# New durations in the cost table of a list schedule, with the instructions kept

## The chip, the cores and the metric

The kernel runs on one core of a Trainium2 chip. The metric is the device time of one execution in microseconds: 1900.26 us is the median of three runs of the kernel before, which lie between 1900.05 and 1903.23 us.

## The reference

The program is a whole network for one batch of 256 tokens of width 1024, all in fp32. The first half has two hybrid layers (in the kernel's names L0 and L1), the second half two blocks of feed-forward nets around a mixer. Cut to what matters:

```python
# each of the two hybrid layers
hx = rms_norm(x, norm_w) * (1 + scale_x) + shift_x           # scale, shift, gate: c_silu @ ada_w
hy = rms_norm(y, norm_w) * (1 + scale_y) + shift_y           # y: 256 tokens of context
p, cp = hx @ w_in, hy @ w_in
ret_x = head_group_norm(bidir_retention(...)) * silu(rg)     # branch r: 4 heads
na_x  = neighbourhood_attention(...) * silu(ng)              # branch n: 8 heads
gqa_x = gqa_blocks(axial_rope(rms_norm(q)), ...) * silu(gg)  # branch g: 8 query heads
x = x + gate_x * ((sig(m0) * (ret_x @ w_ret_o) + sig(m1) * (na_x @ w_na_o)
                   + sig(m2) * (gqa_x @ w_gqa_o)) @ w_out)
y = ...                                                       # the same for the context, layer 0 only
# second half, two blocks: h + 0.5 * swiglu(rms_norm(h)) ; h + mixer(rms_norm(h)) ; the same again
```

## The kernel before

All matrix products are fp32 in three passes: each operand is split into a rounded part and a rest (`split`: a copy on ScalarE makes the rounded part, a subtraction on VectorE the rest), and TensorE multiplies part by part, part by rest and rest by part (`mm3`). A weight comes by DMA into a tile `raw` of 128x2048, and is split into tiles `wh` (ScalarE) and `wl` (VectorE), of which there are four each. Activations lie in 60 tiles `r`, results of TensorE in 8 tiles `ps`, one bank each. The names of tiles begin with a stage and end with a running number: `L0g_r_847` is a tile `r` of branch g in layer 0, `L0m_ps` a sum of the merge of the branches (`m`: gates and output products), `L1r` branch r of layer 1, `ada` the products that give scale, shift and gate, `pro` the start, `f`, `fb`, `fa`, `f0b` and their like the feed-forward nets, `mix` the mixers. The running numbers shift by one or two when the order of recording shifts.

A head or a pair of heads of a branch is a generator (a task). The stages of one in branch g: products for q; the mean of squares by a product with ones; square root on ScalarE, `RECIPROCAL` on VectorE; the scaled q (`SCALAR_TENSOR_TENSOR ...<-L0g_ps,vecs,L0g_r`); a permutation by TensorE (`L0g_ps<-L0g_r,cstt`) and three operations of VectorE that make the rotation; scores; softmax on ScalarE, VectorE and, for the sums over partitions, GpSimd; the split of the probabilities; the product with the values (`L1g_ps<-L1g_r,L1gk_r`).

The order of the program is not the order in which the code is written. Every instruction is recorded first (`record`, line 146), with a duration that `cost` (line 116) works out from its shape. TensorE's durations are also summed into `now`, in the order of recording; a task that says `yield 14` goes on when `now` has moved by 14. Then a list schedule (`schedule`, line 187) makes the order. Each instruction has a due time: where `now` stood when it was recorded, plus 25 for an engine other than TensorE, and never later than the due time of what needs it, less its own duration and 0.6 (line 195). Going through a time of its own, the schedule gives each engine that is free the ready instruction with the earliest due time; an instruction is ready 0.15 after its last source has ended (line 314), and tiles, a ScalarE table that must be loaded (1.28, line 285) and DMAs in flight hold it back as well. `issue` (line 327) emits the instructions in the order so found; line 335, which every row of the profile names, is the call in it. Each engine then works through its own list in that order, and waits on semaphores for what a tile needs.

Of the kernel before, what the change touches and what calls it, by code (L numbers as in the profile page):

```python
# [7 lines left out]
F32 = mybir.dt.float32  # L8
# [87 lines left out]
class _Recorder:  # L96
# [19 lines left out]
    def cost(self, eng, method, out, ins, kw):  # L116
        n = 1
        for e in out.shape[1:]:
            n *= e
        psum = any(i.space == bass.MemoryType.PSUM for i in ins) or out.space == bass.MemoryType.PSUM  # L120
        if eng == "tensor":
            rhs = ins[-1]
            n = 1
            for e in rhs.shape[1:]:
                n *= e
            d = max(n, 64) / 2400.0 * (4 if rhs.dtype == F32 and method == "matmul" else 1) + 0.002
            return d * 0.31 if out.shape[0] == 32 else d
        if eng == "scalar":
            return (n + (61 if psum else 112)) / 1200.0 + 0.093 * (len(ins) - 1)
        if eng == "vector":  # L130
            per = {"reciprocal": 6.0, "tensor_tensor_scan": 2.0}.get(method, 1.0)
            if method == "tensor_scalar" and not psum:
                per = 0.5
            if method == "tensor_reduce":
                n = 1
                for e in ins[0].shape[1:]:
                    n *= e
            return (66 + per * n) / 960.0 + (0.06 if method == "scalar_tensor_tensor" and len(ins) == 3 else 0)
        if eng == "gpsimd":
            return 0.38 + 7.5 * n / 1200.0 if method == "partition_all_reduce" else 0.09 + n / 1200.0  # L140
        b = 4
        for e in out.shape:
            b *= e
        return b / 360e3
# [1493 lines left out]
```

## Time and profile before

| | |
|---|---|
| median of the runs | 1900.26 us |
| profiled execution | 1902.64 us, its span 1900.9 us |
| mean granted TensorE clock | 0.994 |
| TensorE busy | 1858.4 us, 98% of the span |
| VectorE busy | 1432.9 us, 75% |
| ScalarE busy | 1066.3 us, 56%, of it 71.8 us in 56 table loads |
| GpSimd busy | 209.7 us, 11% |
| DMA | 291.95 MB, 152 GB/s read |

A row of a timeline is one instruction or a run of like ones; a number in brackets is the time for which the engine stood idle before it, with the instruction that ended the wait. A windows row gives the busy time of each engine in a stretch, and the granted clock of TensorE in it, where 1.00 is 2.4 GHz and 0.50 is 1.2 GHz.

### The profile page before, as it was taken

Reading aid. Unit: us, or ns where it says so; the run is one execution under the profiler, and the core shown is the slowest. Engines: PE = TensorE matmul, PEld = TensorE weight load, DVE = VectorE, ACT = ScalarE, POOL = GpSimd, SP = SyncE. Lnnn points to the kernel's source line nnn. Section 1 sums busy time; section 2 is a strip of 40 time slices with the busy share of each in tenths; the row PEclk is TensorE's granted clock in tenths of the full one; section 3 lists DMA queues with packets and bytes.
Section 4 is the critical chain, followed back from the end, with each engine's and each line's share of the span. In section 5 each row is a group of like instructions: output and inputs, shape, how many; then the busy total and the mean of one; then the engine's idle time right before and its main releaser. Section 6 shows DMA issues by size and latency. Waiting matters only on the chain.

```text
span 1900.9 us, 33415 instructions
## 1 busy us (share of the span) xinstructions
PE 1858.4 (98%) x13632; PEld 1739.5 (92%) x13632; DVE 1432.9 (75%) x2177; ACT 1066.3 (56%) x1704; POOL 209.7 (11%) x152
## 2 busy tenths in 40 slices
PE   6999999999999999999999999999999999999998
PEld 4888777777789889999999999999999999999998
DVE  7778978799857699999787668876656665777654
ACT  4656555656445597766565447754445444755443
POOL 0123323133300022222000000000000010000000
PEclk9999999999999999999999999999999999999999
DMA  9332443524343324434655566355555555545552
GB/s 321 119 97 93 128 148 101 155 88 123 102 153 100 89 78 116 124 106 146 209 178 188 190 194 200 111 201 187 179 183 180 188 181 193 190 157 176 181 188 98
DMA packets 336249, 291.95 MB, mean 154 GB/s; under 512 B 9184, under 2 KB 325728, under 8 KB 336096
## 3 DMA queue, kind: packets, MB, share of 16 engines
q1 hardware_dynamic: 336096, 289.82, 48.0%
q8 instruction: 107, 1.75, 0.4%
q14 instruction: 46, 0.38, 0.1%
HBM read 288.75 MB, written 1.05 MB: 152 GB/s over the span
## 4 chain that ended last, share of the span: by engine, by line
PE 87%; DVE 8%; ACT 2%; issue 1%; POOL 1%; DMA 0%; SPq 0%; DVEq 0%; POOLq 0%; ACTq 0%
PE fb_ps L335 13%; PE L0m_ps L335 7%; PE f_ps L335 7%; PE fa_ps L335 7%; PE L0n_ps L335 5%; PE L1m_ps L335 5%; PE L1r_ps L335 4%; PE L0r_ps L335 4%; PE fb1b_ps L335 3%; PE L1n_ps L335 3%; PE fa1b_ps L335 3%; PE fb0b_ps L335 3%; PE f0b_ps L335 3%; PE mix_ps L335 3%; PE L0out_ps L335 2%; PE L0in_ps L335 2%
## 5 line engine op out<-in xcount | busy, mean ns | idle before, releaser
L335 PE MATMUL fb_ps<-fb_r,fb_wh 128*128 128x256 f32 x1408 | 253.8, 283 | 0.0
L335 PEld LDWEIGHTS fb_ps<-fb_r,fb_wh 128*128 128x128 f32 x1408 | 219.6, 192 | 0.1
L335 PE MATMUL fb_ps<-fb_r,fb_wl 128*128 128x256 f32 x704 | 198.9, 283 | 0.0
L335 ACT CAST fb_wh<-fb_raw 128x1024 fp32r<-128x1024 f32 x88 | 92.2, 1047 | 123.0 <-PE fb_ps L335 89.3
L335 DVE TENSOR_TENSOR fb_wl<-fb_raw,fb_wh 128x1024 fp32r<-128x1024 f32 x88 | 107.7, 1224 | 65.1 <-ACT fb_wh L335 65.0
L335 PEld LDWEIGHTS fb_ps<-fb_r,fb_wl 128*128 128x128 f32 x704 | 135.0, 192 | 0.0
L335 PE MATMUL f_ps<-f_r,f_wh 128*128 128x256 f32 x704 | 127.2, 283 | 0.0
L335 PE MATMUL fa_ps<-fa_r,fa_wh 128*128 128x256 f32 x704 | 126.9, 283 | 0.0
L335 PE MATMUL L0m_ps<-L0in_r,L0m_wh 128*128 128x512 f32 x384 | 121.5, 395 | 0.0
L335 PEld LDWEIGHTS f_ps<-f_r,f_wh 128*128 128x128 f32 x704 | 109.8, 192 | 0.1
L335 PEld LDWEIGHTS fa_ps<-fa_r,fa_wh 128*128 128x128 f32 x704 | 109.8, 192 | 0.1
L335 PE MATMUL fa_ps<-fa_r,fa_wl 128*128 128x256 f32 x352 | 99.4, 283 | 0.0
L335 PE MATMUL f_ps<-f_r,f_wl 128*128 128x256 f32 x352 | 99.3, 283 | 0.0
L335 PEld LDWEIGHTS L0m_ps<-L0in_r,L0m_wh 128*128 128x128 f32 x384 | 71.9, 189 | 16.7 <-issue 1.6
L335 ACT CAST fa_wh<-fa_raw 128x1024 fp32r<-128x1024 f32 x44 | 46.1, 1047 | 63.5 <-PE fa_ps L335 39.7
L335 DVE TENSOR_TENSOR fa_wl<-fa_raw,fa_wh 128x1024 fp32r<-128x1024 f32 x44 | 53.8, 1224 | 35.4 <-ACT fa_wh L335 35.4
L335 POOL MEMSET mix_r<- 128x128 f32 (+1 forms) x36 | 7.7, 239 | 653.4 <-DVE fa_r L335 490.4
L335 DVE TENSOR_TENSOR L0g_r<-L0g_r,L0g_r 128x512 f32<-128x512 f32 (+3 forms) x116 | 72.4, 670 | 7.6 <-ACT L0g_r L335 5.4
L335 ACT CAST f_wh<-f_raw 128x1024 fp32r<-128x1024 f32 x44 | 46.1, 1048 | 56.4 <-PE f_ps L335 35.6
L335 PE MATMUL L0m_ps<-L0in_r,L0m_wl 128*128 128x512 f32 x192 | 75.0, 391 | 0.0
L335 ACT ACT_TABLE_LOAD x56 | 71.8, 1283 | 3.1 <-PE L0out_ps L335 1.4
L335 DVE TENSOR_TENSOR f_wl<-f_raw,f_wh 128x1024 fp32r<-128x1024 f32 x44 | 53.7, 1221 | 24.9 <-ACT f_wh L335 24.8
(506 smaller groups left out, 5729.7 us busy)
## 6 DMA issues: line engine op xcount, KB each, us to landing
fb_raw<-in_ffn_w_in_dram SPq DMA_DIRECT2D x44, 1024.0 KB, 5.2
f_raw<-in_ffn_w_in_dram SPq DMA_DIRECT2D x22, 1024.0 KB, 5.1
fa_raw<-in_ffn_w_in_dram SPq DMA_DIRECT2D x22, 1024.0 KB, 5.2
ada_raw<-in_ada_w_dram SPq DMA_DIRECT2D x32, 512.0 KB, 4.5
L0m_raw<-in_w_in_dram SPq DMA_DIRECT2D x24, 512.0 KB, 3.9
L1m_raw<-in_w_in_dram SPq DMA_DIRECT2D x24, 512.0 KB, 4.3
L0in_raw<-in_ada_w_dram SPq DMA_DIRECT2D x32, 256.0 KB, 6.0
f0b_raw<-in_ffn_w_out_dram SPq DMA_DIRECT2D x8, 1024.0 KB, 5.3
```

The costliest lines, as they stand in the source:

```text
L335: getattr(getattr(self.real, eng), method)(*a, **k)
```

## The change

Five constants of `cost` change; nothing else does. For TensorE a matmul was reckoned at its columns by 2.4 GHz and 2 ns, and is now reckoned at its columns by 2.4 GHz and 13.5 ns, at least 109 ns: 256 columns go from 0.109 to 0.120, 512 columns from 0.215 to 0.227. An operation of ScalarE gets 118 cycles more on SBUF and 109 more on PSUM, 0.098 and 0.091 us: a copy of 1024 columns goes from 0.947 to 1.045. An operation of VectorE gets 84 cycles more, 0.0875 us: a subtraction of 1024 columns goes from 1.135 to 1.223.

```diff
-            d = max(n, 64) / 2400.0 * (4 if rhs.dtype == F32 and method == "matmul" else 1) + 0.002
-            return d * 0.31 if out.shape[0] == 32 else d
+            if out.shape[0] == 32:
+                return max(n, 64) / 2400.0 * 0.5 + 0.002
+            return max(n / 2400.0 * (4 if rhs.dtype == F32 and method == "matmul" else 1) + 0.0135, 0.109)
         if eng == "scalar":
-            return (n + (61 if psum else 112)) / 1200.0 + 0.093 * (len(ins) - 1)
+            return (n + (170 if psum else 230)) / 1200.0 + 0.093 * (len(ins) - 1)
...
-            return (66 + per * n) / 960.0 + (0.06 if method == "scalar_tensor_tensor" and len(ins) == 3 else 0)
+            return (150 + per * n) / 960.0 + (0.06 if method == "scalar_tensor_tensor" and len(ins) == 3 else 0)
```

The set of instructions stays, but for table loads of ScalarE, 59 where there were 56. Their order moves on every engine, about a third of TensorE's list and more than half of VectorE's.

The first place is VectorE's list in layer 0, around the `RECIPROCAL` of the third group of branch g (`L0g_r_847`). Before:

```order
L335 SCALAR_TENSOR_TENSOR L0m_r_804<-L0m_r_804,L0m_ps_824 128x512
L335 TENSOR_TENSOR L0g_r_820<-L0g_r_820,L0g_r_811 128x256
L335 TENSOR_TENSOR L0m_m_481<-L0m_m_481,L0m_r_804 128x512
L335 TENSOR_TENSOR L0m_wl_865<-L0m_raw_863,L0m_wh_864 128x512
L335 SCALAR_TENSOR_TENSOR L0m_r_829<-L0m_r_829,L0m_ps_832 128x512
L335 RECIPROCAL L0g_r_847<-L0g_r_847 128x512
L335 TENSOR_TENSOR L0m_wl_887<-L0m_raw_884,L0m_wh_886 128x1024
L335 SCALAR_TENSOR_TENSOR L0g_r_848<-L0g_ps_834,vecs,L0g_r_847 128x512
L335 TENSOR_TENSOR L0m_m_495<-L0m_m_495,L0m_r_829 128x512
```

Now:

```order
L336 TENSOR_TENSOR L0g_r_819<-L0g_r_819,L0g_r_810 128x256
L336 TENSOR_TENSOR ada_90<-ada_r_820,vecs 128x8
L336 TENSOR_TENSOR L0g_r_819<-L0g_r_819,L0g_r_810 128x256
L336 RECIPROCAL L0g_r_847<-L0g_r_847 128x512
L336 TENSOR_TENSOR ada_90<-ada_r_820,vecs 128x8
L336 SCALAR_TENSOR_TENSOR L0m_r_803<-L0m_r_803,L0m_ps_824 128x512
L336 SCALAR_TENSOR_TENSOR L0g_r_848<-L0g_ps_834,vecs,L0g_r_847 128x512
L336 TENSOR_TENSOR L0m_m_482<-L0m_m_482,L0m_r_803 128x512
L336 TENSOR_TENSOR L0m_wl_863<-L0m_raw_861,L0m_wh_862 128x512
```

The `RECIPROCAL` stood behind a rest of a weight (`L0m_wl_865`) and two scaled additions of the merge; now it stands right behind the sum of the exponentials of the group before, with two short ada additions at its sides, and the weight's rest behind the scaled q.

The second place is VectorE's list at the end of layer 0, where the last group of branch g is divided by its sums: `L0g_r_1002` is the group's output, `L0g_r_957` (now `L0g_r_955`) the reciprocal of the sums, `L0g_r_1004` the rest of the product that TensorE waits for. Before:

```order
L335 TENSOR_TENSOR L0g_r_1002<-L0g_ps_997,L0g_r_1002 64x512
L335 TENSOR_TENSOR L0m_wl_1019<-L0m_raw_1016,L0m_wh_1018 128x1024
L335 TENSOR_TENSOR L0m_m_709<-L0m_m_709,L0m_r_987 128x512
L335 TENSOR_TENSOR L0m_wl_1022<-L0m_raw_1010,L0m_wh_1021 128x512
L335 RECIPROCAL L0g_r_957<-L0g_r_957 128x512
L335 TENSOR_TENSOR L0g_r_1002<-L0g_ps_1001,L0g_r_1002 64x512
L335 SCALAR_TENSOR_TENSOR L0g_r_957<-L0g_r_957,L0g_r_917 128x512
L335 SCALAR_TENSOR_TENSOR L0m_r_996<-L0m_r_996,L0m_ps_1000 128x512
L335 TENSOR_TENSOR L0g_r_1002<-L0g_r_1002,L0g_r_957 128x512
L335 TENSOR_TENSOR L0m_m_742<-L0m_m_742,L0m_r_996 128x512
L335 TENSOR_TENSOR L0m_wl_1029<-L0m_raw_1026,L0m_wh_1028 128x1024
L335 TENSOR_TENSOR L0g_r_1004<-L0g_r_1002,L0g_r_1003 128x512
```

Now:

```order
L336 TENSOR_TENSOR L0g_r_1002<-L0g_ps_997,L0g_r_1002 64x512
L336 TENSOR_TENSOR L0g_r_1002<-L0g_ps_1001,L0g_r_1002 64x512
L336 TENSOR_TENSOR L0m_wl_1012<-L0m_raw_1010,L0m_wh_1011 128x512
L336 RECIPROCAL L0g_r_955<-L0g_r_955 128x512
L336 SCALAR_TENSOR_TENSOR L0m_r_987<-L0m_r_987,L0m_ps_991 128x512
L336 SCALAR_TENSOR_TENSOR L0g_r_955<-L0g_r_955,L0g_r_915 128x512
L336 TENSOR_TENSOR L0m_m_709<-L0m_m_709,L0m_r_987 128x512
L336 TENSOR_TENSOR L0g_r_1002<-L0g_r_1002,L0g_r_955 128x512
L336 TENSOR_TENSOR L0m_wl_1019<-L0m_raw_1016,L0m_wh_1018 128x1024
L336 TENSOR_TENSOR L0g_r_1004<-L0g_r_1002,L0g_r_1003 128x512
L336 TENSOR_TENSOR L0m_wl_1022<-L0m_raw_1010,L0m_wh_1021 128x512
L336 SCALAR_TENSOR_TENSOR L0m_r_996<-L0m_r_996,L0m_ps_1000 128x512
```

The two rests `L0m_wl_1019` and `L0m_wl_1022` stood ahead of the `RECIPROCAL`; now they stand behind the multiplication, and `L0m_wl_1012` alone stands ahead.

The third place is TensorE's list in layer 1, where the scores of the second group of branch g end (`L1g_ps_1381`) and the first group's product with the values begins (`L1g_ps_1389<-L1g_r_1352,L1gk_r_1309`). Before:

```order
L335 MATMUL L1g_ps_1381<-L1g_r_1358,L1gk_r_1302 128x256
L335 MATMUL L1g_ps_1381<-L1g_r_1356,L1gk_r_1302 128x256
L335 MATMUL L1g_ps_1381<-L1g_r_1358,L1gk_r_1302 128x256
L335 MATMUL L1g_ps_1381<-L1g_r_1356,L1gk_r_1302 128x256
L335 MATMUL L1r_ps_1397<-L0out_r_1156,L1r_wh_1398 128x256
L335 MATMUL L1r_ps_1397<-L0out_r_1157,L1r_wh_1398 128x256
L335 MATMUL L1r_ps_1397<-L0out_r_1156,L1r_wl_1399 128x256
L335 MATMUL L1r_ps_1397<-L0out_r_1159,L1r_wh_1398 128x256
```

Now:

```order
L336 MATMUL L1g_ps_1381<-L1g_r_1358,L1gk_r_1302 128x256
L336 MATMUL L1g_ps_1381<-L1g_r_1356,L1gk_r_1302 128x256
L336 MATMUL L1g_ps_1381<-L1g_r_1358,L1gk_r_1302 128x256
L336 MATMUL L1g_ps_1381<-L1g_r_1356,L1gk_r_1302 128x256
L336 MATMUL L1g_ps_1389<-L1g_r_1352,L1gk_r_1309 128x256
L336 MATMUL L1r_ps_1397<-L0out_r_1156,L1r_wl_1399 128x256
L336 MATMUL L1r_ps_1397<-L0out_r_1159,L1r_wh_1398 128x256
L336 MATMUL L1r_ps_1397<-L0out_r_1160,L1r_wh_1398 128x256
L336 MATMUL L1r_ps_1397<-L0out_r_1159,L1r_wl_1399 128x256
```

Before, 51 matmuls of branch r (`L1r_ps`) stood between the last score and the first product with the values, of which the first four are shown; now that product follows the last score at once, and those of branch r stand behind it.

## Rows read from the trace of the kernel before

**Rows 1.** The page, section 1: busy time, share of the span, instructions.

```profile
PE 1858.4 (98%) x13632; PEld 1739.5 (92%) x13632; DVE 1432.9 (75%) x2177; ACT 1066.3 (56%) x1704; POOL 209.7 (11%) x152
```

**Rows 2.** Waits of PE: what was waited for, total us, times, longest us.

```profile
PE pro_ps L335 <- DVE pro_r L335: 12.3, 1, 12.3
PE L0g_ps L335 <- DVE L0g_r L335: 4.7, 2, 3.6
PE L0m_ps L335 <- ACT L0g_r L335: 3.8, 1, 3.8
PE L1g_ps L335 <- ACT L1g_r L335: 2.9, 3, 1.9
...
PE L0n_ps L335 <- DVE L0n_r L335: 2.0, 3, 1.0
...
PE mix0yb_ps L335 <- DVE mix0y_r L335: 1.0, 1, 1.0
```

**Rows 3.** Chain of waits in order of time: start us, us, what.

```profile
692.67 7.44 PE L1r_ps L335 x51
...
1243.67 127.14 PE fb_ps L335 x1058
```

**Rows 4.** Windows: length; busy us of PE, PEld, DVE, ACT, POOL; PEclk; DMA, GB/s.

```profile
330.00:430.00 100.00, 96.31 (x485) 73.22 (x486) 88.26 (x119) 61.97 (x96) 25.86 (x12) 0.98 0.39 123
430.00:508.00 78.00, 73.12 (x355) 58.79 (x354) 73.81 (x102) 46.51 (x75) 32.37 (x8) 1.00 0.34 101
747.00:894.00 147.00, 145.50 (x1108) 140.06 (x1107) 143.74 (x246) 102.39 (x187) 35.27 (x26) 1.00 0.41 121
326.00:332.00 6.00, 4.53 (x22) 3.51 (x21) 5.94 (x6) 3.19 (x4) 0.00 (x0) 1.00 0.00 0
422.00:426.00 4.00, 4.00 (x21) 2.52 (x14) 4.00 (x4) 0.00 (x0) 0.00 (x0) 0.57 0.97 338
507.50:511.00 3.50, 2.95 (x7) 2.37 (x8) 2.18 (x3) 0.99 (x2) 0.00 (x0) 0.51 0.18 51
690.00:695.00 5.00, 5.00 (x25) 5.00 (x25) 4.34 (x12) 4.31 (x10) 2.43 (x2) 0.50 0.63 176
```

**Rows 5.** Timeline of DVE, 775 to 790 us: start us, us, instruction.

```profile
784.84 1.21 DVE L335 TENSOR_TENSOR L1n_wl<-L1n_raw,L1n_wh 128x1024 fp32r<-128x1024 f32 x1
785.98 0.68 DVE L335 TENSOR_TENSOR L1m_wl<-L1m_raw,L1m_wh 128x512 fp32r<-128x512 f32 x1
```

**Rows 6.** Timeline of ACT, 775 to 790 us.

```profile
782.40 1.05 ACT L335 CAST L1n_wh<-L1n_raw 128x1024 fp32r<-128x1024 f32 x1
783.35 0.61 ACT L335 CAST L1m_wh<-L1m_raw 128x512 fp32r<-128x512 f32 x1
```

**Rows 7.** Timeline of DVE, 409 to 422 us.

```profile
412.74 2.73 DVE L335 TENSOR_TENSOR L0m_wl<-L0m_raw,L0m_wh 128x512 fp32r<-128x512 f32 x1
...
415.99 3.34 DVE L335 RECIPROCAL L0g_r<-L0g_r 128x512 f32<-128x512 f32 x1
...
420.33 0.73 DVE L335 SCALAR_TENSOR_TENSOR L0g_r<-L0g_ps,vecs,L0g_r 128x512 f32<-128x512 f32 x1
```

**Rows 8.** Timeline of PE, 408 to 426 us; in brackets the idle time before.

```profile
421.21 0.67 PE L335 MATMUL L0g_ps<-L0g_r,cstt 128*128 128x256 f32 x2 [3.55 <-DVE L0g_r L335]
```

**Rows 9.** Timeline of DVE, 492 to 512 us.

```profile
501.24 3.33 DVE L335 RECIPROCAL L0g_r<-L0g_r 128x512 f32<-128x512 f32 x1
...
506.66 0.68 DVE L335 TENSOR_TENSOR L0g_r<-L0g_r,L0g_r 128x512 f32<-128x512 f32 x1
```

**Rows 10.** Timeline of PE, 490 to 512 us.

```profile
508.05 0.80 PE L335 MATMUL L0m_ps<-L0g_r,L0m_wh 128*128 128x512 f32 x1 [3.82 <-ACT L0g_r L335]
```

**Rows 11.** Timeline of PE, 692 to 712 us.

```profile
699.95 0.28 PE L335 MATMUL L1g_ps<-L1g_r,L1gk_r 128*128 128x256 f32 x1
```

**Rows 12.** Timeline of ACT, 674 to 702 us.

```profile
684.72 0.58 ACT L335 COPY L1g_r<-L1g_ps 128x512 f32<-128x512 f32 x1
...
698.72 1.13 ACT L335 CAST L1g_r<-L1g_r 128x512 fp32r<-128x512 f32 x2
```

## Prediction

> **What bounds the kernel now.** I read the page first. TensorE is busy for 1858.4 of 1900.9 us, so at most 42.5 us of the span are not its own work [rows 1]. The chain of waits shows where nothing can be won: a feed-forward stretch is 127.14 us for 1058 matmuls of 256 columns, 0.1202 us each with no wait inside [rows 3], and four such stretches and their output halves fill most of the time after 950 us. The order of back-to-back matmuls is worth nothing, so what the change does is decided where TensorE waits. The waits view lists these places [rows 2]: 12.3 us before the first matmul, then branch g of layer 0 (4.7 us in two waits, 3.6 the longest, and 3.8 at its end), branch g of layer 1 (2.9), branch n (2.0) and the first mixer (1.0). The windows add a second price: behind a long wait TensorE's granted clock falls to 1.2 GHz. From 422 to 426 it was 0.57 of full speed, a loss of 0.43 x 4 = 1.7 us of work, and from 507.5 to 511 it was 0.51, again 1.7 us. Behind the 1.47 us that are missing between 326 and 332 (4.53 of 6 us busy) it stayed at 1.00 [rows 4]. So a wait of 3.5 us costs about 5.2, and one of 1.5 costs only itself.
>
> The instructions are the same, so the sum below has only waits in it, read by what stands ahead of what in the new lists, at the durations of the trace.
>
> **First place, third group of branch g in layer 0.** TensorE stands idle for 3.55 us until 421.21, for the scaled q [rows 8]; it had run out of work at 421.21 - 3.55 = 417.66. On VectorE the scaled q starts at 420.33, behind the reciprocal (3.34 us from 415.99) and a weight's rest, and the reciprocal itself starts behind another rest that took 2.73 us from 412.74 [rows 7]. In the new list both rests stand behind the scaled q. From 412.74 to 415.99 are 3.25 us, from the reciprocal's end (415.99 + 3.34 = 419.33) to 420.33 is 1.0: without them the scaled q starts near 420.33 - 4.25 = 416.1, and a scaled addition that now stands in between gives back 0.6. It ends (0.73) near 417.4, before TensorE runs out. The wait goes, and with it the slow stretch: -3.55 - 1.7 = -5.2 us. Bounds: -5.3, and -2 if ScalarE's square root comes later than it did.
>
> **Second place, end of layer 0.** TensorE waits 3.82 us until 508.05 for the split product [rows 10]. On VectorE the reciprocal starts at 501.24 and the multiplication at 506.66 [rows 9]. The new list takes the rests 1019 and 1022 and one scaled addition out of this path, but keeps one other rest in it, and the first addition cannot start before its product is there; I count 1.4 us earlier. TensorE's list has five more matmuls of 512 columns to do meanwhile, at twice the spacing of rows 3 about 1.2 us. So 3.82 - 2.6 = 1.2 us remain, which by the window from 326 to 332 is too little for the clock to fall: -2.6 - 1.7 = -4.3. Bounds: -5.5 (nothing remains), -1.4 (only the path is shorter, the slow stretch stays).
>
> **Third place, first group of branch g in layer 1.** Here the new list looks worse. Before, TensorE did 51 matmuls of branch r, 7.44 us from 692.67 on [rows 3], and reached the first product with the values at 699.95 [rows 11], just when ScalarE's split of the probabilities was done (two copies from 698.72, 1.13 us together) [rows 12]. Now that product comes directly behind the scores, and the 51 matmuls stand behind it. TensorE is in order, so all of them wait with it. VectorE and ScalarE do this group's softmax in one piece now, with three weight rests and a reciprocal behind it, where they were mixed in; the path took 699.95 - 684.72 = 15.2 us [rows 11, 12], and I estimate 2.5 to 4 us less, so the probabilities come between 696 and 697.5. From 692.67 that is 3.3 to 4.8 us of idle time, middle 4. From 690 to 695 the clock was already at 0.50 [rows 4], and most of that falls into the new wait, where it costs nothing (-1.3), while a new slow stretch follows (+1.7): +4 to +5, and I take +4, since the earlier softmax helps the groups behind it. Bounds: -2 (the path becomes so much shorter that even the waits among the scores, 2.9 us, shrink), +9 (no shorter path: 7.44 idle and 1.7 of slow clock).
>
> **The rest.** In branch n of layer 0 one or two fewer weight rests stand ahead of the softmax; the waits are 2.0 in all [rows 2], I take -1 (-2 to +0.5). At the third group of branch g in layer 1 and in the first mixer TensorE's list is between as long as before and 2 us shorter beside the same work of VectorE; waits there are at most 1.0 now [rows 2]. I take +1.5 (0 to +6, the upper end by 7.44 us as for the third place). At the start, eight matmuls move ahead of the first result and four small VectorE operations go behind: 0 (-0.5 to +0.7). Three more table loads on ScalarE, at 56% busy [rows 1], are hidden by its idle time; where one falls into a softmax path, it is inside the bounds above.
>
> Sum: -5.2 - 4.3 + 4 - 1 + 1.5 + 0 = -5.0 us. The profiled execution took 1902.6 us, its span and 1.7 around it, and lies 2.4 above the median of the runs, at the top of their spread; taken from the median, 1900.3 - 5.0 = 1895.3 us.
>
> **Are the new durations better?** For TensorE the trace says yes: 0.1202 us from matmul to matmul [rows 3], where the table had 0.109 and now has 0.120. For the others it depends on what is meant. A rest of 1024 columns on VectorE shows 1.21 us, but the next instruction starts 785.98 - 784.84 = 1.14 after it [rows 5]; a copy on ScalarE shows 1.05, the next starts 0.95 later [rows 6]. The table had 1.135 and 0.947, and now has 1.223 and 1.045: it has left the spacing, and taken up the time until a result can be used.
> The Trainium skill, page "Perfetto Trace Analysis", section "Optimizing Scalar/DVE Operations", says the same against this change: the cost per instruction that occupies the engine is about 60 ns on VectorE and 93 ns on ScalarE from SBUF, and the profiled latency holds about twice that, because the second half overlaps with the next instruction. The trace agrees here (0.07 and 0.10 us of overlap). By that rule the plan now books too much time on VectorE, as in the second rival below; by the rows of the three places the sum stays.
>
> **Rivals.** *The third place costs nothing* (1891): the softmax path becomes 7 us shorter, so that the product with the values is ready when the scores end. The sum without the +4 is -9. For it: rows 12 have 14 us between the first and the last step on ScalarE, for operations of about half a microsecond each. Against: VectorE was busy for 4.34 of 5 us in the stretch [rows 4].
>
> *Softmax first, TensorE empty* (1905, the slower side): the plan books VectorE 7% too long per rest and more for short operations; from 747 to 894 VectorE is busy for 143.7 of 147 us [rows 4], so it takes VectorE for the bound and draws each softmax forward, ahead of the rests that TensorE's filling work needs. If the third place costs its upper bound of 9 and the next group its 6, while the rest of the sum stands at -10.5, the result is +4.5. It decides when layer 1 loses over 14 us more than now. For it: 51 matmuls moved at one place. Against: the places where TensorE's list got shorter are few, and the second is a matter of 1 to 2 us.
>
> *The stalls only move* (1901): in layer 0 VectorE is busy for 88.3 of 100 us and then for 73.8 of 78 [rows 4]; what is put behind a reciprocal must be done soon, and a weight's rest that comes late stops TensorE too. If layer 0 keeps 4 to 5 us of its 9.5, the sum is about +0.5. Against: the waits of layer 0 are few and long [rows 2], not spread over the stage as they would be if VectorE were its bound.
>
> **How the numbers follow.** Runs of this kernel cannot tell a change of under 0.2%, 3.8 us, from none. The forecast has a chance of 0.42, with its own range from -9 to -1; two thirds of that are faster by over 3.8. The free third place has 0.18, softmax first 0.18, the moving stalls 0.22. Faster: 0.28 + 0.18 = 0.46; same: 0.14 + 0.21 = 0.35; slower: 0.18 + 0.01 = 0.19. The range goes from 1885.5, where the lower bounds of several places meet (-2 at the third place, -5.3, -5.5, -2), to 1906, a little over the slower rival.
>
> **What would show it.** Right: no wait over 1.5 us of `L0g_ps` for VectorE near 417 and of `L0m_ps` for ScalarE near 505, no stretch at half clock there, and a new wait of 3 to 5 us in layer 1 before the first product with the values, followed by half clock; the feed-forward stretches unchanged at 0.1202 us per matmul. Wrong: if waits of the old length stand at other places of layer 0, if the new wait in layer 1 is 7 us or none, or if a place that I have not named (branch n, the projections for layer 1) waits for over 3 us.

## The result, and the profile after

The changed kernel takes 1924.86 us, median of four runs (1923.43 to 1925.50). With a fourth run of 1903.18 us the median of the kernel before is 1901.72 us. The ratio is 1.0121, with a 95% interval from 1.0103 to 1.0138. That is 23 us slower, where 5 us faster was forecast, and outside the range. The profiled execution has a span of 1923.1 us, 22.2 more than before.

The page, section 1, of the changed kernel. TensorE's matmuls are the same, so against [rows 1] all of the time is in waits and in slow clock: TensorE is busy for 12.2 us more, at a mean granted clock of 0.986 instead of 0.994, and idle for 52.5 instead of 42.5 us.

```profile
PE 1870.6 (97%) x13632; PEld 1747.4 (91%) x13632; DVE 1434.8 (75%) x2177; ACT 1071.9 (56%) x1707; POOL 200.2 (10%) x152
```

TensorE's waits in the changed kernel (what was waited for: total us, times, longest us), to be held against [rows 2]:

```profile
PE L1g_ps L336 <- ACT L1g_r L336: 5.5, 1, 5.5
PE L0m_ps L336 <- DVE L0m_wl L336: 4.2, 5, 1.9
PE L1m_ps L336 <- ACT L1r_r L336: 3.8, 1, 3.8
PE mix0yb_ps L336 <- ACT mix0y_r L336: 3.5, 1, 3.5
...
PE L1n_ps L336 <- DVE L1n_r L336: 2.3, 1, 2.3
PE L0g_ps L336 <- DVE L0g_r L336: 1.9, 3, 0.9
PE L0m_ps L336 <- DVE L0m_r L336: 1.9, 1, 1.9
...
PE L0m_ps L336 <- ACT L0g_r L336: 0.2, 1, 0.2
```

The two long waits of layer 0 are gone (`L0g_ps` for VectorE has 0.9 as its longest instead of 3.6, `L0m_ps` for ScalarE 0.2 instead of 3.8). What stands in the list instead was shorter or absent before: waits for rests of weights and for VectorE's additions in layer 0, a wait of 5.5 us in branch g of layer 1 (1.9 was the longest), one of 3.8 for branch r's result, one of 2.3 in branch n, and 3.5 us in the first mixer.

The chain of waits in order of time (start us, us, what) says where the 22 us lie. These are picked rows, with the rows between them left out; first the changed kernel, then the kernel before. The rows of a pair begin at the same point of TensorE's work: as many matmuls lie ahead of them in both traces.

```profile
295.01 1.00 PE ada_ps L336 x16
478.27 16.15 PE L0m_ps L336 x71
570.67 46.49 PE L0out_ps L336 x386
669.21 1.43 PE L1r_ps L336 x12
733.88 12.68 PE L1r_ps L336 x84
869.73 14.40 PE L1m_ps L336 x120
993.56 127.56 PE f_ps L336 x1060
1265.00 127.14 PE fb_ps L336 x1058
```

```profile
289.73 1.00 PE ada_ps L335 x16
474.89 16.32 PE L0m_ps L335 x72
567.50 46.49 PE L0out_ps L335 x386
664.74 1.43 PE L1r_ps L335 x12
724.18 12.71 PE L1r_ps L335 x84
849.77 14.40 PE L1m_ps L335 x120
973.38 127.56 PE f_ps L335 x1060
```

The difference of a pair is how far the changed kernel is behind at that point:

| point | behind, us | since the point before, us | what lies between |
|---|---|---|---|
| 295.01 | 5.3 | +5.3 | the start, branch n of layer 0 |
| 478.27 | 3.4 | -1.9 | the first place, most of branch g of layer 0 |
| 570.67 | 3.2 | -0.2 | the second place |
| 669.21 | 4.5 | +1.3 | the beginning of layer 1 |
| 733.88 | 9.7 | +5.2 | the third place |
| 869.73 | 20.0 | +10.3 | the rest of branch g, branch r's result, branch n of layer 1 |
| 993.56 | 20.2 | +0.2 | the end of layer 1 |
| 1265.00 | 21.3 | +1.2 | the first mixer ([rows 3] have its pair, 1243.67) |

Layer 0 ends 3.2 us later, layer 1 takes 17.0 us more (422.9 from its start to the first feed-forward stretch instead of 405.9), and 2.0 come after that, most of it at the first mixer. A feed-forward stretch takes 127.14 us for 1058 matmuls, as in [rows 3].

TensorE's timeline of the changed kernel at the third place, and at two places further on in layer 1 (picked rows):

```profile
702.60 0.58 PE L336 MATMUL L1g_ps<-L1g_r,L1gk_r 128*128 128x256 f32 x1 [5.51 <-ACT L1g_r L336]
...
774.64 1.04 PE L336 MATMUL L1m_ps<-L1r_r,L1m_wh 128*128 128x256 f32 x2 [3.80 <-ACT L1r_r L336]
...
831.59 0.74 PE L336 MATMUL L1n_ps<-L1n_r,L1n_r 128*128 128x256 f32 x4 [2.30 <-DVE L1n_r L336]
```

The windows of the changed kernel (length; busy us of PE, PEld, DVE, ACT, POOL; PEclk; DMA, GB/s): first the stretch that held a slow stretch before, then the five slow stretches of the two layers. The last row, apart, is of the kernel before, the slow stretch around its 690 to 695.

```profile
330.00:430.00 100.00, 98.02 (x477) 75.97 (x476) 85.89 (x114) 64.15 (x99) 25.35 (x12) 1.00 0.33 102
217.90:224.70 6.80, 5.81 (x17) 4.85 (x18) 6.77 (x7) 2.16 (x3) 4.67 (x4) 0.50 0.26 77
504.50:508.00 3.50, 3.44 (x8) 2.78 (x9) 3.44 (x6) 0.00 (x0) 0.00 (x0) 0.52 0.62 180
692.50:706.00 13.50, 7.55 (x32) 6.96 (x33) 12.06 (x25) 11.98 (x23) 2.65 (x4) 0.50 0.20 57
774.40:781.00 6.60, 6.36 (x28) 6.10 (x29) 6.60 (x13) 6.60 (x13) 0.00 (x0) 0.50 0.44 128
832.40:839.10 6.70, 6.11 (x28) 6.11 (x29) 5.86 (x11) 1.74 (x3) 3.08 (x5) 0.50 0.32 94
```

```profile
688.60:695.20 6.60, 5.89 (x27) 5.89 (x28) 5.40 (x15) 5.91 (x14) 2.43 (x2) 0.50 0.57 159
```

From 330 to 430, where a slow stretch cost 1.7 us before, the clock is 1.00. But TensorE works for 29.3 us at half clock in these five stretches, and half of that, 14.6 us, is lost. Before, it worked for 12.1 us at half clock in three stretches (3.3 and 2.9 behind the waits at 421 and 508, [rows 4], and the 5.9 of the last row), a loss of 6.1. So the slow clock is more than a third of what the layers lose.

### The profile page after: what moved, and what is told of

Same layout as the page of the kernel before. It is cut to its first block, busy times and chain, and to the rows that moved or that the text cites. A ratio compares the mean times of both kernels' runs of the same rounds, so it can differ in the third digit from the quotient of the medians.

```text
span 1923.1 us, 33416 instructions
## 1 busy us (share of the span) xinstructions
PE 1870.6 (97%) x13632; PEld 1747.4 (91%) x13632; DVE 1434.8 (75%) x2177; ACT 1071.9 (56%) x1707; POOL 200.2 (10%) x152
## 4 chain that ended last, share of the span: by engine, by line
PE 89%; DVE 5%; ACT 3%; issue 1%; DMA 1%; POOL 0%; SPq 0%; DVEq 0%; ACTq 0%; POOLq 0%
PE fb_ps L336 13%; PE L0m_ps L336 8%; PE f_ps L336 7%; PE fa_ps L336 7%; PE L0n_ps L336 5%; PE L1m_ps L336 5%; PE L1n_ps L336 4%; PE L0r_ps L336 4%; PE L1r_ps L336 4%; PE fb1b_ps L336 3%; PE fa1b_ps L336 3%; PE fb0b_ps L336 3%; PE f0b_ps L336 3%; PE L0g_ps L336 3%; PE mix_ps L336 3%; PE L0out_ps L336 2%
## 5 line engine op out<-in xcount | busy, mean ns | idle before, releaser
L336 DVE TENSOR_TENSOR L0g_r<-L0g_r,L0g_r 128x256 f32<-128x256 f32 (+3 forms) x116 | 76.8, 709 | 8.8 <-ACT L0g_r L336 7.9
L336 ACT CAST L0m_wh<-L0m_raw 128x1024 fp32r<-128x1024 f32 (+1 forms) x48 | 39.9, 836 | 66.9 <-PE L0m_ps L336 29.7
```

What stands on the lines that cost most here:

```text
L336: getattr(getattr(self.real, eng), method)(*a, **k)
```

## The experiments

Theories at the start: A, the longer durations of VectorE and ScalarE draw the softmax paths ahead of TensorE's filling work; B, TensorE's new durations disturb the clock of recording, on which the pauses count; C, the greedy schedule answers any other numbers with another set of waits. D, E and F came up on the way.

**Parts of the change, each alone.** The edits are the hunks of the diff: TensorE's, both of the others, and one each.

> Only TensorE's new durations; VectorE and ScalarE as before. Theory A (the longer VectorE and ScalarE durations pull the softmax paths ahead of TensorE's filling work): 1890 to 1900 us, no new wait over 3 us in layer 1. Theory B (TensorE's durations also drive the recording clock, on which the tasks' pauses count, and that breaks the stagger of the tasks): 1915 to 1925, with the same long waits as the changed kernel. Theory C (the greedy schedule answers any change of numbers with another set of waits): 1895 to 1920, with long waits at other places than the changed kernel has.

Measured: 1921.7 us, ratio 1.0096 (1.0081 to 1.0111).

> Only the new durations of VectorE and ScalarE; TensorE as before. Theory A: 1915 to 1925 us, with the wait of over 5 us before the first product with the values in layer 1. Theory B: 1895 to 1903. Theory C: 1895 to 1920, and the difference to before does not add up with that of TensorE's part alone to the 23 us of the whole.

Measured: 1924.2 us, 1.0110 (1.0093 to 1.0127).

> Only VectorE's new durations. Theory A: 1908 to 1925 us, since VectorE is the engine that the plan takes for the bound. Theory B: 1895 to 1903. Theory C: anywhere from 1895 to 1920, and not between the kernel before and the one with both VectorE and ScalarE changed.

Measured: 1934.4 us, 1.0166 (1.0150 to 1.0181).

> Only ScalarE's new durations. Theory A: 1898 to 1908 us, less than VectorE's part. Theory B: 1895 to 1903. Theory C: anywhere from 1895 to 1920.

Measured: 1916.7 us, 1.0070 (1.0055 to 1.0085).

Each part alone costs 14 to 32 us, and VectorE's and ScalarE's together 22, less than VectorE's alone. A is refuted by e1, and B by e2. A gave the time of e2, but put a wait of over 5 us into layer 1, where the longest is 3.7. C is right that the parts don't add up and that the longest waits lie at other places each time (with TensorE's part alone 5.2 us for VectorE in branch g of layer 0, with ScalarE's alone 6.8 us in the first mixer), but three of the four times lie above its range. TensorE's part holds one thing more than the columns: products of TensorE with 32 rows of output (`ada`), booked at 0.034 us for 256 columns before, are booked at 0.055 now.

**How little is enough.** The kernel before, with one number of the plan moved by next to nothing.

```diff
# p1_dve1
-            return (66 + per * n) / 960.0 + (0.06 if method == "scalar_tensor_tensor" and len(ins) == 3 else 0)
+            return (67 + per * n) / 960.0 + (0.06 if method == "scalar_tensor_tensor" and len(ins) == 3 else 0)
# p3_pe
-            d = max(n, 64) / 2400.0 * (4 if rhs.dtype == F32 and method == "matmul" else 1) + 0.002
+            d = max(n, 64) / 2400.0 * (4 if rhs.dtype == F32 and method == "matmul" else 1) + 0.0025
```

> The kernel before, with one cycle (0.001 us) more on each VectorE operation in the plan, a number that carries no knowledge; some 29 rows of TensorE's list and 43 of VectorE's move, the names left aside. Theory C (the order before is a chosen one among scattered ones, and any change of numbers leaves it): slower by 3 us or more. Theory A (wrong proportions between the engines' durations do the harm): within 2 us of before, since no proportion changes.

Measured: 1903.6 us, 1.0006 (0.9997 to 1.0016).

> The kernel before, with 0.0005 us more on each matmul in the plan; some 146 rows of TensorE's list and 130 of VectorE's move. Theory C: slower by 5 to 25 us, like the changed kernel, though the durations are as wrong as they were. Theory A: within 2 us of before, or faster, since it is a step of one part in twenty towards TensorE's measured spacing.

Measured: 1907.9 us, 1.0029 (1.0017 to 1.0041).

p3 costs 5 us, though its number is nearer to the trace; p1 cannot be told from none, and there C is wrong. More rows moved doesn't mean more lost, either. Counted from the profiles (rows outside the longest common order, the tiles' numbers left aside), VectorE's list moves in 47 rows in p1, 130 in p3 and 394 in the changed kernel; in f3 below it moves in 292 and the time stays, and in g2 below it moves in 434 and the time falls by 15 us. So a small step can lose and a large one need not. By the same count the changed kernel moves 532 of TensorE's 13632 rows and 394 of VectorE's 2177: far fewer than the third and the half that I gave with the change.

**Where it is lost.** All new durations, for the instructions of one layer alone.

```diff
-        op.dur = self.cost(eng, method, out, ins, kw)
+        op.dur = (self.cost_new if out.tensor.name[:2] == "L1" else self.cost)(eng, method, out, ins, kw)
```

> All new durations, for the instructions of layer 1 alone; the others keep the old ones. The prediction's account (the loss of the changed kernel is made in layer 1, mainly before the first product with the values): 1912 to 1922 us, layer 1 longer by some 15, layer 0 as before. Theory C: 1900 to 1920, with long waits at other places of layer 1 than the changed kernel has.

Measured: 1916.6 us, 1.0078 (1.0063 to 1.0093). TensorE's waits of this kernel (total us, times, longest us):

```profile
PE L1g_ps L366 <- ACT L1g_r L366: 5.8, 2, 5.5
PE L0g_ps L366 <- DVE L0g_r L366: 4.7, 2, 3.5
PE L0m_ps L366 <- ACT L0g_r L366: 3.8, 1, 3.8
PE L1m_ps L366 <- ACT L1r_r L366: 3.8, 1, 3.8
PE L1n_ps L366 <- DVE L1n_r L366: 2.8, 2, 2.3
```

Layer 0's two old waits are back, and layer 1 has the changed kernel's: 5.5, 3.8, 2.3. This settles the place: the numbers of layer 1 alone make these waits, with layer 0's two old waits ahead of them, and cost 14 us. C, which asked for waits at other places, is wrong here.

> All new durations, for the instructions of layer 0 alone. The prediction's account (the two long waits of layer 0 go, 9.5 us with their slow clock): 1891 to 1897 us. Theory C: the two waits shrink, and waits elsewhere take back as much or more, 1898 to 1920.

Measured: 1907.0 us, 1.0023 (1.0013 to 1.0032). Its longest waits in layer 0:

```profile
PE L0m_ps L366 <- DVE L0m_wl L366: 3.8, 4, 2.1
PE L0n_ps L366 <- ACT L0n_r L366: 3.3, 1, 3.3
...
PE L0g_ps L366 <- DVE L0g_wl L366: 3.0, 1, 3.0
```

The two old waits are gone, as forecast, and branch n and rests of weights that come late take back more than they were worth.

**What the numbers book.** Theory D starts from [rows 5, 6]: the new durations of VectorE and ScalarE hold 0.07 to 0.10 us in which the next instruction already runs. f1 takes that out of the engines' time and lengthens the delay until a result can be used; f2 has the delay alone, g1 the engines' time alone, f3 the delay in the kernel before.

```diff
-_LAT = 0.15
+_LAT = 0.25              # f1; 0.3 in f2 and f3; unchanged in g1
...
                     end = at[e] = start + op.dur
+                    if e in ("scalar", "vector"):      # f1 and g1
+                        at[e] -= 0.09
```

> The changed kernel with two edits in the plan: VectorE and ScalarE are free for the next instruction 0.09 us before the end that the new durations give (the spacing that the traces show), and a result is ready 0.25 instead of 0.15 after its end. Theory D (the new durations book as occupied engine what the trace shows as overlap with the next instruction, and the delay until a result can be used is too short in the plan): 1886 to 1898 us, faster than the changed kernel by over 25. Theory C (any other numbers scatter the order and lose): 1910 to 1930.

Measured: 1909.7 us, 1.0044 (1.0027 to 1.0061).

> The changed kernel, with the delay of a result alone set from 0.15 to 0.30. Theory D: 1910 to 1922 us, since the engines' occupied time is still too long; the delay alone doesn't mend it. Theory C: 1905 to 1930, no telling. If the delay were all, it would come below 1903.

Measured: 1923.4 us, 1.0115 (1.0099 to 1.0130).

> The changed kernel, with VectorE and ScalarE free for the next instruction 0.09 us earlier in the plan, and nothing else. Theory D (occupied time booked too long): 1905 to 1916 us, at least 8 faster than the changed kernel. If the plan's other constants are all that matters: 1918 to 1930.

Measured: 1921.1 us, 1.0098 (1.0083 to 1.0113).

> The kernel before, with the delay of a result alone set from 0.15 to 0.30. Theory D: 1894 to 1902 us, since VectorE's and ScalarE's durations there are the spacing already and the delay gets nearer to the truth. Theory C: 1908 to 1925, since the order leaves the one that it had.

Measured: 1901.8 us, 0.9998 (0.9988 to 1.0007).

Both edits together win back 15 of 23 us, less than D asked. Each alone wins 1.5 to 4, and the intervals of f2 and g1 overlap with the changed kernel's, so neither is told from it for certain. At the third place f1's longest wait is 1.42 us, where the changed kernel had 5.51. The plan of f1 still loses 8 us against the kernel before, and D's forecasts missed for f1, f2 and g1; only that for f3 came true. With the 0.09 taken off, f1 books for VectorE and ScalarE nearly what the old table did; it is close to TensorE's part alone (e1, 1921.7 us) with a longer delay. That the 15 us come from booking the overlap right, and not from one more other order, is not shown.

**The plan's other constants.** Were these only tuned beside the old numbers? f4, g2 and g3 share another set, chosen for the numbers of f4; they have TensorE's new durations alone, all old ones, and all new ones.

```diff
-CAP = 25
+CAP = 36
-AHEAD = 60
+AHEAD = 50
-LATK = 0.6
+LATK = 0.5
-SWITCH = 4
+SWITCH = 3
-ADAY, ADAZ = 4, 40
+ADAY, ADAZ = 2, 30
-_LAT = 0.15
+_LAT = 0.3
-                live[k][1] = nc.now + next(live[k][0])
+                live[k][1] = nc.now + 1.05 * next(live[k][0])
```

> TensorE's new durations, VectorE's and ScalarE's old ones (the spacing), a delay of 0.30, and the plan's other constants chosen anew for these numbers: 36 for 25 as the due time of the other engines, 0.5 for 0.6 in the due times, pauses longer by 5%, look-ahead 50 for 60, table switch 3 for 4, ada's pauses 2 and 30 for 4 and 40. Theory D: 1878 to 1890 us, with at most two waits of over 2 us after the start. Theory C: 1905 to 1925.

Measured: 1898.3 us, 0.9981 (0.9972 to 0.9990).

> The kernel before with the other constants of f4_best: all old durations. Theory D: 1895 to 1903 us, a little over f4_best (1898.3), since only TensorE's spacing is wrong. If the constants are all that matters: the same as f4_best, within 3.

Measured: 1887.8 us, 0.9920 (0.9903 to 0.9936).

> The changed kernel with the other constants of f4_best: all new durations. Theory D: 1905 to 1920 us, clearly over f4_best and the old durations beside the same constants. If the constants are all that matters: 1895 to 1902, like f4_best.

Measured: 1904.7 us, 1.0009 (1.0000 to 1.0019).

The constants are worth 15 to 20 us with either table, and the table is worth about as much with either set: all new against all old is 23 us beside the old constants and 1904.7 - 1887.8 = 17 us beside the new ones. So the loss is not bound to the one set that stood beside the old table. A set chosen for the new table by runs was not tried, and may still favour it. g2, with the old durations, is the fastest of all, 15 us faster than the kernel before; its longest wait after the start is 2.0 us, in branch g of layer 0. None of the times forecast for f4, g2 and g3 came true; that g3 lies clearly over the two others did.

**The proportion between the engines.** Theory E: the old table was short by about a tenth on all engines, so that their proportion was right (VectorE to TensorE 0.786 in the plan's sums; 1432.9 to 1858.4, or 0.771, by [rows 1]); the new one has 0.832. h1 and h2 keep TensorE's new durations and scale the others, beside the old and the new constants (VectorE to TensorE 0.789).

```diff
-        op.dur = self.cost(eng, method, out, ins, kw)
+        op.dur = self.cost(eng, method, out, ins, kw) * (1.085 if eng in ("vector", "scalar") else 1.0)
```

> TensorE's new durations, and the old ones of VectorE and ScalarE times 1.085: VectorE's sum is then 1435 us, by the trace 1433. Theory E (the proportion between the engines decides): 1898 to 1908 us, at least 12 faster than TensorE's part alone. Theory C (any order off the old one loses some 14 to 30): 1912 to 1925.

Measured: 1918.5 us, 1.0082 (1.0067 to 1.0097).

> The same beside the new set of the other constants. Theory E: 1884 to 1892 us, like the old durations beside that set (1887.8) and faster than f4_best (1898.3). Theory C: 1894 to 1908, scattered between f4_best and the all-new durations.

Measured: 1898.4 us, 0.9978 (0.9968 to 0.9988).

E falls: both are where TensorE's part alone was (1921.7 and 1898.3).

**The clock of recording.** Theory F, which is B taken by itself.

```diff
-            self.now += op.dur
+            self.now += self.new         # TensorE's new duration; op.dur stays the old one
```

> TensorE's new durations in the recording clock alone (pauses and due times); in the plan itself all durations are the old ones. Theory F (the clock that spaces the tasks and the due times does the harm): 1915 to 1925 us, like TensorE's part as a whole (1921.7). If it is TensorE's taken time in the plan: 1898 to 1906.

Measured: 1930.2 us, 1.0149 (1.0132 to 1.0165).

TensorE's new numbers in the recording clock alone cost 28 us, more than the whole change and more than F asked. There a pause of 14 stood for 14 / 0.1087 = 129 matmuls of 256 columns and now stands for 14 / 0.1202 = 116, and all due times move apart by a tenth, while 25 and 0.6 stay. So this clock alone is enough to lose more than TensorE's part (19 us). That e1 loses in this way is not shown: e5's longest wait after the start is 2.9 us, in branch g of layer 1, e1's is 5.2, in branch g of layer 0. And it does not explain the other half: in e2 this clock is the old one, and 22 us are lost all the same. Pauses lengthened in step with the clock were not tried by themselves.

## Why the prediction was wrong

**The first place** was right: no wait of `L0g_ps` in layer 0 is over 0.9 us, and the slow stretch behind it is gone (1.00 from 330 to 430). The times of the step hold when they are counted from TensorE, which is some 6 us later here (timelines of DVE and of PE):

```profile
422.78 0.75 DVE L336 SCALAR_TENSOR_TENSOR L0g_r<-L0g_ps,vecs,L0g_r 128x512 f32<-128x512 f32 x1
```

```profile
423.58 0.70 PE L336 MATMUL L0g_ps<-L0g_r,cstt 128*128 128x256 f32 x2
```

The scaled q ends at 423.53, just before TensorE reaches it. The margin is 0.05 us where 0.3 was reckoned, so there was some luck in it. From 295 to 478 the kernel gains 1.9 us all the same, and not 5.2: smaller losses around the place take back the rest.

**The second place** failed. The forecast was -4.3; from 478 to the end of layer 0 the kernel gains 0.2. Of the old wait 0.17 us are left, but 10 us ahead of it TensorE now waits 1.90 us for a scaled addition of the merge. The slow stretch, which was to go, is still there, in front of the old wait instead of behind it: 0.52 from 504.5 to 508. The timelines of DVE, POOL and PE show what came in (picked rows):

```profile
500.53 2.25 DVE L336 TENSOR_SCALAR ada<-ada 128x16 f32<-128x16 f32 x1
502.70 0.67 DVE L336 SCALAR_TENSOR_TENSOR L0m_r<-L0m_r,L0m_ps 128x512 f32<-128x512 f32 x1
```

```profile
500.51 3.23 POOL L336 PARTITION_ALL_REDUCE L0g_r<-L0g_r  x1 [1.93 <-DVE ada L336]
```

```profile
503.43 0.74 PE L336 MATMUL L0m_ps<-L0g_r,L0m_wh 128*128 128x512 f32 x2 [1.90 <-DVE L0m_r L336]
...
513.65 0.49 PE L336 MATMUL L0m_ps<-L0g_r,L0m_wh 128*128 128x512 f32 x1 [0.17 <-ACT L0g_r L336]
```

A short ada operation of 16 columns takes 2.25 us beside GpSimd's sum over partitions, the scaled addition behind it is late, and TensorE waits for that addition. The step had looked at the path of the last group alone, and at nothing else that TensorE needs from VectorE in that stretch.

**The third place** was right in kind. It was forecast at +4 and measured +5.2. TensorE stands empty for 5.51 us; I said 3.3 to 4.8. What was off is "2.5 to 4 us less", in one piece, for the softmax path: ScalarE's timeline in the changed kernel has

```profile
688.28 1.24 ACT L336 COPY L1g_r<-L1g_ps 128x512 f32<-128x512 f32 x2
...
697.96 1.04 ACT L336 CAST L1r_wh<-L1r_raw 128x1024 fp32r<-128x1024 f32 x1
...
699.33 1.28 ACT L336 ACT_TABLE_LOAD   x1
```

From the first copy to the product with the values are 702.60 - 688.28 = 14.3 us, against 15.2 before: 0.9 less. A weight's copy (1.04 us) and a table load (1.28) still stand in the path.

**The step that turned the sign is "the rest"**, with +0.5 us for all that was not one of the three places. By the table it measured about +19: 5.3 at the start and in branch n of layer 0, where -1 was forecast; 1.3 at the beginning of layer 1; 10.3 from 734 to 870; and 2.2 behind that. To it come the 4.1 us that the second place didn't give and the smaller losses around the first. I had read the new lists at the places where TensorE waits now, and taken the others at what they wait now ("waits there are at most 1.0 now"). Waits arose at places that had cover before: for a rest of a weight at 219, for branch r's result at 774, for branch n's at 831, each over 1.8 us. I had called a wait of over 3 us at a place not named a sign of being wrong; the one at 774, of 3.80, is such a place. The runs with one layer's numbers say the same: e8_L0 shows the exchange in layer 0 by itself, e7_L1 the loss in layer 1.

**The price of a wait** was too low as well. Each slow stretch stood at 1.7 us in the sum; those at 774 and 832 cost 3.2 and 3.1 (half of 6.36 and 6.11 us of work), and in the two layers there are five where there were three.

**The rivals.** "Softmax first" named the layer and its point of decision: layer 1 would lose over 14 us, and it lost 17. It had 0.18, and its time of 1905 kept layer 0's gain, which was not to be had. "The stalls only move" was right for layer 0, which kept nothing of its 9.5. What the trace said on the durations (0.07 and 0.10 us of overlap) was used for the rival "softmax first" and not for the forecast. The Trainium skill's rule, in page "Perfetto Trace Analysis", section "Optimizing Scalar/DVE Operations", was used in the same way. f1, which takes the overlap out of the booked time and puts it into the delay, wins 15 us back, so it may have deserved more weight.

**What stays open.** It is shown where the time goes, that layer 1's own numbers make layer 1's waits, and that each part of the change alone, and the recording clock alone, is enough to lose. Why the old table orders better than the new one beside two sets of constants is not: neither proportion nor delay nor occupied time is enough for it, and it may be chance of a greedy order, of which two draws are few.

## What to carry to other kernels

A list schedule is not improved by truer durations as such: twelve kernels here have some of the new durations beside one of the two sets of other constants, and none was faster than the old table beside the same set. When an order moves in hundreds of rows, a forecast from the waits of the old order counts the gains and misses the losses, since a place that was covered can become uncovered; look at the covered places too, and leave the upper end of the range open for them. What the engine is booked for and when its result can be used are two numbers; f1, which keeps them apart, is the best of the four kernels with all new durations and the old due times and pauses, though that this is the reason is not shown. Numbers that also drive another clock (pauses, due times) change what is counted on it; here that alone cost 28 us.

## What the runs showed of the hardware

A VectorE operation can be held up beside GpSimd's sums over partitions. In the second place above an operation of 16 columns took 2.25 us, where the median of its form is 0.17; in [rows 7] the rest that took 2.73 us, where another of its size takes 0.68 [rows 5], lies beside this sum (timeline of POOL, kernel before):

```profile
412.41 3.50 POOL L335 PARTITION_ALL_REDUCE L0g_r<-L0g_r  x1 [2.22 <-DVE L0g_r L335]
```

It is one operation at a time and not all of them. Of VectorE's 2177 operations in the changed kernel 40 take more than 1.5 times the median of their form (forms that occur at least five times); all 40 lie beside one of the 72 sums over partitions, never two beside the same, and together they are 44 us longer than their medians. In the kernel before it is 41 operations and 43 us. So most of the 2.73 us of [rows 7] was not that rest's own, and moving the rest does not take the delay out of VectorE's time. In the changed kernel one of these delays fell on the short ada operation, at a place where TensorE needed what came next. The plan has no such term in either table, nor had the prediction.

TensorE's clock fell behind shorter waits than the 3.5 us of the prediction. In the changed kernel it was at half around a wait of 1.87 us that ended at 218.89 (0.50 from 217.9 to 224.7), and behind one of 1.90 us that ended at 503.43 and one of 0.40 just after (0.52 from 504.5 to 508). In the kernel before it had been so behind 1.86 us that ended at 687.95 and 0.85 just after (0.50 from 688.6 to 695.2), while the 1.47 us of [rows 4] left it at 1.00.
